# Token slots of 1024 columns in place of 1032, and pools shifted to multiples of 256 bytes, in a decoder layer on one Trainium2 core

## The chip, the core and the metric

The kernel runs on one core of one Trainium2 chip. The metric is the time of one execution on the device in microseconds (us); the time of a kernel is the median of its runs.

## What is computed

One decoder layer in float32 over 512 tokens of 2048 values, with weights that are used once each. The reference, cut to its frame:

```python
mod_all = einsum('bd,ldm->lbm', silu(c), w_ada) + b_ada        # six vectors of 2048
h = modulate(rms_norm(x, norm1_g), sh1, sc1)
u = h @ w_in                                                   # conv, queries, six key/value parts, gates
y_conv = short_conv_mixer(u_b, u_c, u_h, conv_w, conv_b)
k_cmp = compress(kv_heads(kc, True), cmp_pe_k, cmp_w1_k, cmp_w2_k)
v_cmp = compress(kv_heads(vc, False), cmp_pe_v, cmp_w1_v, cmp_w2_v)
y_attn = nsa_attention(q, k_cmp, v_cmp, k_slc, v_slc, k_win, v_win, gates)
mixed = concat([rms_norm(y_conv, gnorm_conv_g), rms_norm(y_attn, gnorm_attn_g)])
x = x + g1 * (mixed @ w_out)
h = modulate(rms_norm(x, norm2_g), sh2, sc2)
x = x + g2 * (square(relu(h @ w_ff1)) @ w_ff2)                 # 8192 hidden values
return rms_norm(x, normf_g)
```

`compress` turns windows of 32 tokens, 16 apart, into one key or value each: 31 windows, each a vector of 32 x 128 values, times a 4096 x 256 matrix, a gelu, and a 256 x 128 matrix.

## The kernel before

**Split matmuls.** Each float32 operand is held as two parts, `hi` (a rounded copy, made by ScalarE) and `lo` (the remainder, made by VectorE). `mm3` (L338) multiplies such a pair by another in three matmuls: hi by hi, hi by lo, lo by hi. For weights the parts are called `wh` and `wl`, or the two halves of a tile `hl`. In every matmul the weights, a 128 x 128 block, are loaded into the array by their own instruction, and the tokens, 512 or 256 columns, stream past.

**Stages.** The front (L344 to L871) computes the modulation vectors (192 loads of 512 KB, `wa`, each multiplied and summed on VectorE), the projections of `w_in`, the convolution and the compression. Its tokens stand in 16 tiles of 128 partitions: the first seven in the pool `side` (`h`), nine in slots (`h_m`). Weights come as raw blobs of 128 x 1024, or 128 x 1072 for the value projection, into three staging tiles `raw`, and are split into two pairs `wh`, `wl` by `weights` (L325). The attention stage (L874 to L1032) works on 8 heads and four blocks of 128 queries, with the output projection of the convolution half between, and ends with the first two blocks `w_oa`, staged the same way. The feed-forward stage (L1035 to the end) finishes the output projection and computes the two large matmuls by seven products on half blocks instead of eight, with 256 token columns in each matmul. It loads raw blobs into six tiles `rw` of 4096 bytes per partition and splits them into three tiles `hl` of 8192, two `sg` of 4096, or into `gt`. Its token tiles `tk` are slots again: in the first half of the stage the same 28 tiles serve all blocks; in the second half 14 new ones are loaded from DRAM for each of eight parts.

**Memory.** SBUF is handed out as a stack of pools, each tile padded to 32 bytes per partition. From the bottom: 16,512 bytes of scratch and constants of the framework, `consts` (`vec` of 1344 bytes first), `small`, then `mainp` with its 29 slots, each 128 x 1032 float32, 4128 bytes per partition. The slots begin at byte 34464 and end at 154176. Above come `attc` (`cst`, `ident_r`, `mask_r`, `kslc`, `vcmp` and small tiles, in the order in which the code makes them), `stage` (first three `raw` of 4288 bytes, then two `wh` and two `wl` of 4288) and `side`, whose place the pool `pa` takes in the attention stage. When `attc`, `stage` and `pa` are closed, the feed-forward's pool `ffp` starts at 154176, in the same bytes: six `rw`, three `hl` from 178752, `sg`, `gt`, `gb`, `p1`. A tile laid over an older one waits until the older one is done with. Seen modulo 256, the slots start at 160, 192, 224, 0, 32 and so on in turn, `hl`, `sg` and `gt` at 64, the two pairs `wh`, `wl` at (64, 192) and (0, 128), the side tiles `h` at 64.

**Order.** The class `Order` (L43) records all instructions of a stage, prices each by its operation and width, and plans in which order every engine issues them; a slot is given to the next tile when its last user is done. DMAs of weights are issued on SP's queue in that order. Tiles of the feed-forward are written by the same order with its own plan.

**Compression.** `compress` (L685) puts the 32 positions of all windows into two tiles `ct`, one for positions 0 to 15 and one for 16 to 31, each column group of 64 being the windows of both key/value groups for one position. It splits each into `chi` and `clo` and multiplies position after position. A weight load takes 66 columns, `m = slice((l % 16) * 64, (l % 16) * 64 + 66)`, and at the last position of a tile the two columns beyond the 1024 are read; the slot's columns 1024 to 1031 are set to zero for that (L691).

Of the kernel before, what the change touches and what calls it, by code (L numbers as in the profile page):

```python
# [9 lines left out]
F32 = mybir.dt.float32  # L10
F32R = mybir.dt.float32r
# [5 lines left out]
P = 128  # L17
T = 512
# [3 lines left out]
NG = 2  # L22
# [4 lines left out]
NEG = -1e30  # L27
SCALE = HD ** -0.5
BLOB = 1072
SLOT = 1032  # L30
NMAIN = 29
NSIDE = 7
NWA = 8
# [3 lines left out]
V_BADA, V_N1, V_CW, V_CB, V_GC, V_GA, V_N2, V_NF, V_C, V_ID, V_END = \  # L37
    0, 96, 112, 136, 144, 152, 160, 176, 192, 208, 336
C_COS, C_SIN, C_MASK, C_CMASK, C_ROW, C_END = 0, 512, 1024, 1152, 1280, 1281
# [230 lines left out]
def hybrid_layer(ctx: ExitStack, tc: tile.TileContext, a, out):  # L270
    nc = tc.nc
    PSUM = bass.MemoryType.PSUM

    consts = ctx.enter_context(tc.tile_pool(name="consts", bufs=1))
# [4 lines left out]
    attc = front.enter_context(tc.tile_pool(name="attc", bufs=1))  # L279
    stage = front.enter_context(tc.tile_pool(name="stage", bufs=2))  # L280

    def slot(dtype=F32, name="m"):
        return mainp.tile([P, SLOT], dtype, name=name, tag="m")

    def pair(dtype=F32, name="m"):
        return slot(dtype, name)[:, :2 * T].rearrange("p (a b) -> p a b", a=2)

    xs = [pair(name="x2") for _ in range(NK // 2)]
    nc = order = Order(tc, xs[0].tensor.tag, NMAIN, passes=6)
    ts = [small.tile([P, T], F32, name="t", tag="t", bufs=5) for _ in range(5)]  # L290
    scr, temps = ts[0].bitcast(BF16), cycle(ts[1:])
    accums = cycle([small.tile([P, T], F32, name="sacc", tag="acc2k", bufs=2) for _ in range(2)])
    wraw = cycle([stage.tile([P, BLOB], F32, name="raw", bufs=3) for _ in range(3)])
    whl = cycle([[stage.tile([P, BLOB], F32R, name=n) for n in ("wh", "wl")] for _ in range(2)])
    accs = cycle([small.tile([P, 2], F32, name="acc") for _ in range(4)])

    def temp(shape=(P, T), dtype=F32, name=None):
        t = next(temps)[:, :math.prod(shape[1:])].bitcast(dtype)
        if len(shape) == 4:
            return t.rearrange("p (a b c) -> p a b c", b=shape[2], c=shape[3])  # L300
        return t if len(shape) == 2 else t.rearrange("p (a b) -> p a b", b=shape[2])
# [23 lines left out]
    def weights(src, cols=1024, spare=False):  # L325
        raw = next(wraw)[:, :cols]
        nc.sync.dma_start(out=raw, in_=src)
        wh, wl = (slot(F32R, name="sw") for _ in range(2)) if spare else next(whl)
        wh, wl = wh[:, :cols], wl[:, :cols]
        nc.scalar.activation(wh, raw, AF.Copy)  # L330
        nc.vector.tensor_tensor(out=wl, in0=raw, in1=wh.bitcast(F32), op=OP.subtract)
        return wh, wl

    def split(dst, src):
        nc.scalar.activation(dst[:, 0], src, AF.Copy)
        nc.vector.tensor_tensor(out=dst[:, 1], in0=src, in1=dst[:, 0].bitcast(F32), op=OP.subtract)

    def mm3(ps, lh, ll, rh, rl, start, stop, more=False):  # L338
        nc.tensor.matmul(ps, lh, rh, start=start, stop=False, skip_group_check=more)
        nc.tensor.matmul(ps, lh, rl, start=False, stop=False, skip_group_check=more)  # L340
        nc.tensor.matmul(ps, ll, rh, start=False, stop=stop, skip_group_check=more)


    vec = consts.tile([P, V_END], F32, name="vec")  # L344
    nc.sync.dma_start(out=vec, in_=a["vec"][:, :V_END])
    ident = vec[:, V_ID:V_END]
    for i in range(NK // 2):
        nc.sync.dma_start(out=xs[i], in_=a["xt"][i])
    cst = attc.tile([P, C_END - C_MASK], F32, name="cst")
    cmask = cst[:, C_CMASK - C_MASK:C_ROW - C_MASK].rearrange("p (b n) -> p b n", b=NQ)  # L350
    rowv = cst[:, C_ROW - C_MASK:]
    ident_r = attc.tile([P, P], F32R, name="ident_r")
    mask_r = attc.tile([P, P], F32R, name="mask_r")
    rot = pair(name="rot")
    cos, sin = rot[:, 0], rot[:, 1]
    ones = consts.tile([P, P], F32, name="ones")
# [164 lines left out]
        yield 0.65  # L521

    kc, kwin = [], []
    kslc = [attc.tile([P, 2, 32 + T], F32R, name=f"kslc{g}") for g in range(NG)]

    def keys():

# [55 lines left out]
    for s, (name, k) in enumerate(steps[:-1]):  # L583
# [5 lines left out]
        wh, wl = w  # L589
# [50 lines left out]
    def other():  # L640
        return next(others)
# [36 lines left out]
        return ps  # L678


    vcmp = attc.tile([P, NG, 2, P], F32R, name="vcmp")
    cw2 = pair(name="cw2").rearrange("p a b -> p (a b)")[:, :576]
    nc.sync.dma_start(out=cw2, in_=a["vec"][:, V_END:])

    def compress(which, src):  # L685
        pe = cw2[:, which * 32:which * 32 + 32]
        w2 = [cw2[:, 64 + (which * 2 + i) * P:64 + (which * 2 + i + 1) * P] for i in range(2)]
        parts = []
        for hf in range(2):
            t = slot(name="ct")  # L690
            nc.vector.memset(t[:, 1024:SLOT], 0.0)  # L691
            tv = t[:, :1024].rearrange("p (l g n) -> p l g n", g=NG, n=32)
            n = 32 - hf
            for g in range(NG):
                nc.vector.tensor_tensor(
                    out=tv[:, :, g, :n],
                    in0=src[g].rearrange("p (n l) -> p l n", l=16)[:, :, hf:],
                    in1=pe[:, hf * 16:hf * 16 + 16, None].to_broadcast([P, 16, n]), op=OP.add)
            if hf:
                nc.vector.memset(tv[:, :, :, 31:], 0.0)  # L700
            hi = slot(F32R, name="chi")
            lo = slot(F32R, name="clo")
            nc.scalar.activation(hi, t, AF.Copy)
            nc.vector.tensor_tensor(out=lo, in0=t, in1=hi.bitcast(F32), op=OP.subtract)
            parts.append((hi, lo))
            if hf:
                w = weights(a["cmp_w1"][which * 8], spare=True)
            yield
        pc = other()
        for blk in range(8):  # L710
            wh, wl = w
            hi, lo = parts[blk // 4]
            for j in range(4):
                l = blk * 4 + j
                s = slice(j * 256, (j + 1) * 256)
                m = slice((l % 16) * 64, (l % 16) * 64 + 66)
                mm3(pc[:66, :256], hi[:, m], lo[:, m], wh[:, s], wl[:, s], l == 0, l == 31)
            if blk < 7:
                w = weights(a["cmp_w1"][which * 8 + blk + 1], spare=True)
            yield  # L720
        hid = temp([P, 256], name="hid")[:64]
        tt = temp([P, 256], name="htt")[:64]
        nc.scalar.activation(hid, pc[:64, :256], AF.Copy)
        nc.vector.tensor_tensor(out=tt, in0=hid, in1=hid, op=OP.mult)
        nc.vector.tensor_scalar(tt, tt, 0.044715, 1.0, op0=OP.mult, op1=OP.add)
        nc.vector.tensor_tensor(out=tt, in0=tt, in1=hid, op=OP.mult)
        nc.scalar.activation(tt, tt, AF.Tanh, scale=math.sqrt(2.0 / math.pi))
        nc.vector.tensor_scalar(tt, tt, 1.0, 0.5, op0=OP.add, op1=OP.mult)
        nc.vector.tensor_tensor(out=hid, in0=hid, in1=tt, op=OP.mult)
        pt = other()  # L730
        for i in range(2):
            nc.tensor.transpose(pt[:, i * 64:i * 64 + 64], hid[:, i * P:(i + 1) * P], ident[:64, :64])
        hidt = temp([P, 2, NG, 32], name="hidt")
        nc.scalar.activation(hidt.rearrange("p i g n -> p (i g n)"), pt[:, :P], AF.Copy)
        yield
        if which == 0:
            pk = other()
            for i in range(2):
                nc.tensor.matmul(pk[:, :64], w2[i], hidt[:, i].rearrange("p g n -> p (g n)"),
                                 start=i == 0, stop=i == 1)  # L740
            for g in range(NG):
                split(kslc[g][:, :, :32], pk[:, g * 32:g * 32 + 32])
        else:
            pad = temp([P, 2, NG, P], name="hpad")
            nc.vector.memset(pad, 0.0)
            nc.vector.tensor_copy(pad[:, :, :, :32], hidt)
            for g in range(NG):
                pv = other()
                for i in range(2):
                    nc.tensor.matmul(pv[:, :P], pad[:, i, g], w2[i], start=i == 0, stop=i == 1)  # L750
                split(vcmp[:, g], pv[:, :P])
# [6 lines left out]
    for j in range(8):  # L758
# [4 lines left out]
        for i in range(3):  # L763
            n = 3 * j + i
# [30 lines left out]
    for g in range(NG):  # L795
        pv = [bank() for _ in range(NQ)]
        for blk in range(4):
            wh, wl = weights(a["w_v"][g * 4 + blk], BLOB)
            more_ada(1)
            for j in range(4):  # L800
                k = blk * 4 + j
                s = slice(j * 268, (j + 1) * 268)
# [43 lines left out]
    for g in range(NG):  # L846
        pq = [bank() for _ in range(NR)]
        for k in range(NK):
            if k % 2 == 0:
                wh, wl = weights(a["w_q"][g * 8 + k // 2])  # L850
                more_ada(1)
                tick()
            for n in range(NR):
                s = slice((k % 2 * NR + n) * P, (k % 2 * NR + n + 1) * P)
# [28 lines left out]
    nc = tc.nc  # L883
    temps = cycle(ts)
    nc = order = Order(tc, mix[0].tensor.tag, NMAIN, passes=6)
# [113 lines left out]
    m = 2  # L999
# [35 lines left out]
    nc = order = Order(tc, x1[0].tensor.tag, NMAIN)  # L1035
# [57 lines left out]
    for k in range(8):  # L1093
        wh, wl = oa[k] if k < 2 else hilo(hl_tile(), raw_blob(a["w_oa"][k]))
        for i in range(8):
            s = slice(i * P, (i + 1) * P)
# [309 lines left out]
    for f in range(8):  # L1406
# [7 lines left out]
        for q in range(3 if last else 4):  # L1414
            raw = [raw_blob(a["w_f2"][4 * f + q, b]) for b in range(4)]
            ps = [{}, {}]
            for i, w in enumerate(operands(raw)):
# [3 lines left out]
                for j in range(2):  # L1421
                    mp = 2 * q + j
                    m = 2 * mp
# [119 lines left out]
```

## Time and profile before

| | |
|---|---|
| median of 3 runs | 2165.89 us |
| lowest and highest of them | 2164.7 and 2166.03 us |
| span of the profiled execution | 2163.4 us |

The span runs from the first instruction to the last of one profiled execution; the times of the runs hold what lies around it too. A page of the profile gives the busy time of each engine, then groups of instructions: the tile written, the tiles read, the shape, the count, the busy time and the mean length of one. All instructions that `Order` records carry its line, L116, so groups are told apart by the names of their tiles. Matmuls overlap: one of 512 columns is listed with some 0.39 us, one of 256 with 0.28, and the next starts before it ends. Their pace is therefore read from their starts, or from a count in a stretch. PE is TensorE's matmuls, PEld its weight loads, DVE VectorE, ACT ScalarE, POOL GpSimd, SP the engine that issues most DMAs.

### The profile page before, as it was taken

How to read it: one execution, taken by the hardware profiler on the slowest of the kernel's cores; microseconds unless marked ns; L12 is line 12 of the kernel's file. 1: busy time of each engine (PE TensorE's matmuls, PEld its weight loads, DVE VectorE, ACT ScalarE, POOL GpSimd, SP SyncE). 2: the span in 40 equal slices, each digit the busy share in tenths (PEclk: the TensorE clock that was granted, in tenths of full speed). 3: DMA queues.
4: the chain of work that ended last, by engine and by line, in shares of the span. 5: the costliest groups of instructions: out<-in, count | busy, mean ns of one | idle time of the engine just before them, and what ended most of it. 6: DMA issues, size and time to landing. Idle time of an engine off the chain costs nothing.

```text
span 2163.4 us, 37948 instructions
## 1 busy us (share of the span) xinstructions
PE 2107.7 (97%) x15014; PEld 1956.2 (90%) x15014; DVE 1891.8 (87%) x2975; ACT 1009.7 (47%) x1470; POOL 128.6 (6%) x244
## 2 busy tenths in 40 slices
PE   5999999999999999999999999999999999999997
PEld 3888777898777779999999999999999999999997
DVE  8989988887887547999999999999899999999997
ACT  4532333222555435766656665666433333333344
POOL 0000000000000001021112111111000000000000
PEclk8999999999999999999999999999999999999998
DMA  8996678888220144476666666668875366366342
GB/s 330 341 345 223 232 285 317 314 292 292 78 88 30 59 159 158 137 228 193 193 212 197 195 198 212 192 196 284 315 278 212 139 239 233 125 242 234 134 179 88
DMA packets 144129, 454.16 MB, mean 210 GB/s; under 512 B 15824, under 2 KB 20176, under 8 KB 143952
## 3 DMA queue, kind: packets, MB, share of 16 engines
q1 hardware_dynamic: 108816, 386.72, 50.1%
q0 software_dynamic: 34048, 63.98, 9.6%
q8 instruction: 118, 1.93, 0.4%
q10 hardware_dynamic: 1088, 1.05, 0.1%
q14 instruction: 59, 0.48, 0.1%
HBM read 383.53 MB, written 68.16 MB: 209 GB/s over the span
## 4 chain that ended last, share of the span: by engine, by line
PE 87%; DVE 7%; DMA 3%; issue 1%; ACT 1%; SPq 0%; DVEq 0%; ACTq 0%
PE pf L116 61%; PE ps L116 20%; PE pw L116 3%; PE pv L116 1%; DVE t L116 1%; DMA raw<-in_cmp_w 1%; PE s L116 1%; PE pt L116 1%; DVE nm L116 1%; DMA raw<-in_w_conv 1%; DVE wl L116 1%; DVE x L116 1%; DVE hl L116 1%; DVE p L116 0%; DMA rw<-in_w_f 0%
## 5 line engine op out<-in xcount | busy, mean ns | idle before, releaser
L116 PE MATMUL pf<-tk,hl 128*128 128x256 f32 x10704 | 1264.6, 280 | 1.2 <-DVE hl L116 0.7
L116 PEld LDWEIGHTS pf<-tk,hl 128*128 128x128 f32 x10704 | 1262.8, 188 | 1.8 <-DVE hl L116 0.9
L116 ACT ACTIVATE hl<-rw 128x1024 fp32r<-128x1024 f32 x269 | 284.7, 1059 | 354.6 <-PE pf L116 339.0
L116 DVE TENSOR_TENSOR hl<-rw,hl 128x1024 fp32r<-128x1024 f32 x269 | 327.9, 1220 | 52.2 <-ACT hl L116 52.1
L116 ACT ACTIVATE hl<-sg 128x1024 fp32r<-128x1024 f32 x180 | 191.1, 1062 | 247.5 <-PE pf L116 233.3
L116 DVE SCALAR_TENSOR_TENSOR t<-wa,cs 128x1024 bf16<-128x1024 f32 x192 | 234.5, 1221 | 21.7 <-DMA wa<-in_w_ada 19.2
L116 ACT ACTIVATE wh<-raw 128x1024 fp32r<-128x1024 f32 (+1 forms) x106 | 112.7, 1064 | 261.0 <-PE ps L116 222.1
L116 PE MATMUL ps<-h_m,wh 128*128 128x512 f32 x720 | 226.8, 394 | 0.0
L116 DVE TENSOR_TENSOR hl<-sg,hl 128x1024 fp32r<-128x1024 f32 x151 | 184.4, 1221 | 35.1 <-ACT hl L116 34.9
L116 PE MATMUL ps<-h,wh 128*128 128x512 f32 x560 | 179.4, 400 | 5.2 <-ACT h L116 3.2
L116 PEld LDWEIGHTS ps<-h_m,wh 128*128 128x128 f32 x720 | 134.8, 188 | 30.8
L116 DVE SCALAR_TENSOR_TENSOR x<-pf,mod,x 128x256 f32<-128x256 f32 (+1 forms) x280 | 134.6, 487 | 18.5 <-PE pf L116 17.8
L116 DVE TENSOR_TENSOR wl<-raw,wh 128x1024 fp32r<-128x1024 f32 (+1 forms) x106 | 129.9, 1226 | 23.3 <-ACT wh L116 22.8
L116 DVE TENSOR_TENSOR sg<-sg,rw 128x1024 f32<-128x1024 f32 x120 | 146.1, 1217 | 0.1
L116 PE MATMUL ps<-h_m,wl 128*128 128x512 f32 x360 | 141.8, 394 | 0.0
L116 PEld LDWEIGHTS ps<-h,wh 128*128 128x128 f32 x560 | 107.0, 192 | 32.7 <-ACT h L116 5.2
L116 POOL DMA_DIRECT2D g<-gt x192 | 101.5, 533 | 364.5 <-issue 179.2
L116 PE MATMUL ps<-h,wl 128*128 128x512 f32 x280 | 111.8, 399 | 0.0
L116 PE MATMUL pw<-mix,wh 128*128 128x512 f32 x256 | 86.7, 404 | 0.0
L116 PEld LDWEIGHTS ps<-h_m,wl 128*128 128x128 f32 x360 | 67.6, 188 | 15.8
L116 ACT ACTIVATE t<-t 128x512 f32<-128x512 f32 (+3 forms) x131 | 74.6, 571 | 13.0 <-DVE t L116 11.0
L116 DVE TENSOR_TENSOR sg<-rw 128x1024 f32<-128x1024 f32 x60 | 73.1, 1218 | 6.1 <-DMA rw<-in_w_f 3.2
(216 smaller groups left out, 2151.7 us busy)
## 6 DMA issues: line engine op xcount, KB each, us to landing
rw<-in_w_f SPq DMA_DIRECT2D x263, 512.0 KB, 3.8
wa<-in_w_ada SPq DMA_DIRECT2D x192, 512.0 KB, 6.2
tk<-g SPq DMA_DIRECT2D x114, 512.0 KB, 6.4
g<-gt POOLq DMA_DIRECT2D x192, 256.0 KB, 3.4
raw<-in_w_conv SPq DMA_DIRECT2D x32, 512.0 KB, 4.4
x<-in_xt SPq DMA_DIRECT2D x16, 512.0 KB, 6.1
raw<-in_w_kv SPq DMA_DIRECT2D x16, 512.0 KB, 4.9
raw<-in_w_cv SPq DMA_DIRECT2D x16, 512.0 KB, 3.6
```

Source lines behind the costliest of these rows:

```text
L116: x.i, x.eng, x.call = len(self.nodes), eng, (lambda: real(*args, **kw))
```

## The change

`SLOT` becomes 1024 columns, 4096 bytes. `vec` is padded from 336 to 424 columns, so that the slots begin at byte 34816, a multiple of 1024, and end at 153600. `kslc`, `vcmp`, `ident_r` and `mask_r` are made first in `attc`, `cst` is padded to 337 columns, staged tiles become 1088 columns wide (4352 bytes) of which 1072 are used, and `wh` and `wl` are made ahead of `raw`. With that `stage` begins at 169472 and the side tiles at 199936, both multiples of 256; `ffp` begins at 153600 and `hl` at 178176, multiples of 1024.

In `compress` the two columns past the end are no longer there: the memset goes, the copies take 1024 columns, and at positions 15 and 31 the weight load takes 64 columns and the matmul writes 64 rows instead of 66. In each block of four positions the last two change places, so that the accumulation ends with a position of 66 rows.

```diff
-SLOT = 1032
+SLOT = 1024
+WIDE = 1088
+VEC_W = 336 + 88
+CST_W = 1281 - 1024 + 80
...
-    wraw = cycle([stage.tile([P, BLOB], F32, name="raw", bufs=3) for _ in range(3)])
-    whl = cycle([[stage.tile([P, BLOB], F32R, name=n) for n in ("wh", "wl")] for _ in range(2)])
+    kslc = [attc.tile([P, 2, 32 + T], F32R, name=f"kslc{g}") for g in range(NG)]
+    vcmp = attc.tile([P, NG, 2, P], F32R, name="vcmp")
+    ident_r = attc.tile([P, P], F32R, name="ident_r")
+    mask_r = attc.tile([P, P], F32R, name="mask_r")
+    whl = cycle([[stage.tile([P, WIDE], F32R, name=n)[:, :BLOB] for n in ("wh", "wl")] for _ in range(2)])
+    wraw = cycle([stage.tile([P, WIDE], F32, name="raw", bufs=3)[:, :BLOB] for _ in range(3)])
...
-    vec = consts.tile([P, V_END], F32, name="vec")
+    vec = consts.tile([P, VEC_W], F32, name="vec")[:, :V_END]
...
-    cst = attc.tile([P, C_END - C_MASK], F32, name="cst")
+    cst = attc.tile([P, CST_W], F32, name="cst")[:, :C_END - C_MASK]
...
-            nc.vector.memset(t[:, 1024:SLOT], 0.0)
-            tv = t[:, :1024].rearrange("p (l g n) -> p l g n", g=NG, n=32)
+            tv = t.rearrange("p (l g n) -> p l g n", g=NG, n=32)
...
-            for j in range(4):
+            for j in (0, 1, 3, 2):
                 l = blk * 4 + j
                 s = slice(j * 256, (j + 1) * 256)
-                m = slice((l % 16) * 64, (l % 16) * 64 + 66)
-                mm3(pc[:66, :256], hi[:, m], lo[:, m], wh[:, s], wl[:, s], l == 0, l == 31)
+                rows = 66 if l % 16 < 15 else 64
+                m = slice((l % 16) * 64, (l % 16) * 64 + rows)
+                mm3(pc[:rows, :256], hi[:, m], lo[:, m], wh[:, s], wl[:, s], l == 0, l == 30)
```

More of the change, by code (lines that the diff above doesn't have):

```diff
@@ L348, in hybrid_layer @@
         nc.sync.dma_start(out=xs[i], in_=a["xt"][i])
-    cst = attc.tile([P, C_END - C_MASK], F32, name="cst")
+    cst = attc.tile([P, CST_W], F32, name="cst")[:, :C_END - C_MASK]
     cmask = cst[:, C_CMASK - C_MASK:C_ROW - C_MASK].rearrange("p (b n) -> p b n", b=NQ)
     rowv = cst[:, C_ROW - C_MASK:]
-    ident_r = attc.tile([P, P], F32R, name="ident_r")
-    mask_r = attc.tile([P, P], F32R, name="mask_r")
     rot = pair(name="rot")
@@ L523, in hybrid_layer @@
     kc, kwin = [], []
-    kslc = [attc.tile([P, 2, 32 + T], F32R, name=f"kslc{g}") for g in range(NG)]
     def keys():
@@ L678, in project @@
         return ps
-    vcmp = attc.tile([P, NG, 2, P], F32R, name="vcmp")
     cw2 = pair(name="cw2").rearrange("p a b -> p (a b)")[:, :576]
```

## The prediction, made before the change was run

> **What bounds the kernel now.** I read the page's busy line and its chain of work that ended last, then the view of stretches for the stages, then single stretches of TensorE's order of time.
>
> ```profile
> span 2163.4 us, 37948 instructions
> ...
> PE 2107.7 (97%) x15014; PEld 1956.2 (90%) x15014; DVE 1891.8 (87%) x2975; ACT 1009.7 (47%) x1470; POOL 128.6 (6%) x244
> ...
> PE 87%; DVE 7%; DMA 3%; issue 1%; ACT 1%; SPq 0%; DVEq 0%; ACTq 0%
> PE pf L116 61%; PE ps L116 20%; PE pw L116 3%; PE pv L116 1%; DVE t L116 1%; DMA raw<-in_cmp_w 1%; PE s L116 1%; PE pt L116 1%; DVE nm L116 1%; DMA raw<-in_w_conv 1%; DVE wl L116 1%; DVE x L116 1%; DVE hl L116 1%; DVE p L116 0%; DMA rw<-in_w_f 0%
> ```
>
> The reader is to see that 87% of the chain is TensorE itself, and that 61% is one group, the feed-forward matmuls into `pf`. The stretches below (busy time and count of PE, PEld, DVE, ACT, POOL, then clock, DMA share, GB/s) show it busy without a gap, at the full granted clock:
>
> ```profile
> 100.00:150.00 50.00, 50.00 (x217) 40.42 (x216) 44.77 (x79) 21.72 (x30) 0.00 (x0) 1.00 0.91 338
> ...
> 1000.00:1500.00 500.00, 500.00 (x4241) 500.00 (x4240) 455.93 (x609) 309.42 (x431) 94.69 (x179) 1.00 0.65 204
> ...
> 1560.00:2150.00 590.00, 589.08 (x4996) 588.64 (x4995) 551.56 (x789) 238.97 (x270) 2.64 (x5) 1.00 0.53 191
> ```
>
> 500 us over 4241 matmuls is 117.9 ns from start to start; 590 us over 4996 is 118.1. So the time is the number of matmuls times their pace, and only what changes the pace or the number can move it much. The groups, with their counts:
>
> ```profile
> L116 PE MATMUL pf<-tk,hl 128*128 128x256 f32 x10704 | 1264.6, 280 | 1.2 <-DVE hl L116 0.7
> ...
> L116 PE MATMUL ps<-h_m,wh 128*128 128x512 f32 x720 | 226.8, 394 | 0.0
> ...
> L116 PE MATMUL ps<-h,wh 128*128 128x512 f32 x560 | 179.4, 400 | 5.2 <-ACT h L116 3.2
> ...
> L116 PE MATMUL ps<-h_m,wl 128*128 128x512 f32 x360 | 141.8, 394 | 0.0
> ...
> L116 PE MATMUL ps<-h,wl 128*128 128x512 f32 x280 | 111.8, 399 | 0.0
> ...
> L116 PE MATMUL pw<-mix,wh 128*128 128x512 f32 x256 | 86.7, 404 | 0.0
> ```
>
> **Part 1, the pace: what addresses do to it.** The change keeps these matmuls and moves their operands. Before, a token slot is 4128 bytes, so the 29 slots start at all eight multiples of 32 modulo 256, while the feed-forward weight blocks (`hl`, `sg`, `gt`) start at 64 modulo 256 every time. Call *offset* the address of a token tile minus that of the weights, modulo 256. Here are runs of six matmuls on one token slot (columns: start, us from first start to last end, group, count):
>
> ```profile
> 1072.48 0.84 PE L116 MATMUL pf<-tk,hl 128*128 128x256 f32 x6
> 2063.69 0.84 PE L116 MATMUL pf<-tk,hl 128*128 128x256 f32 x6
> 1521.20 0.88 PE L116 MATMUL pf<-tk,hl 128*128 128x256 f32 x6
> 2118.88 0.88 PE L116 MATMUL pf<-tk,hl 128*128 128x256 f32 x6
> 900.37 0.86 PE L116 MATMUL pf<-tk,hl 128*128 128x256 f32 x6
> 938.66 0.87 PE L116 MATMUL pf<-tk,hl 128*128 128x256 f32 x6
> 2147.49 0.88 PE L116 MATMUL pf<-tk,sg 128*128 128x256 f32 x6
> ```
>
> One matmul lasts 0.28, so five steps take 0.56 in the first two rows and 0.60 in the next two: 112 and 120 ns by rounded figures, 113.3 and 120.0 by the trace's starts. Clock, shape and engine are alike; the slots differ. The first pair is the first and last of 26 runs at offset 192 in which every step is 113.3. The second is the first and last of 24 runs at offset 0 (slot 5) in which, after a first step of 117, every step is 120.0. Rows six and seven are the first and last of all 228 runs at offset 0 (slots 5, 13, 21). Over all 1754 runs of six (900.37 the first, 2147.49 the last), the steps behind the first average, by offset: 0 118.7; 32 117.7; 64 117.6; 96 119.4; 128 119.5; 160 118.0; 192 116.2; 224 118.5.
>
> It is the offset and not the token address alone. In the projections two weight buffers alternate, at (`wh`, `wl`) = (0, 128) and (64, 192) modulo 256. First and last start of three blocks of 24 matmuls:
>
> ```profile
> 110.43 0.62 PE L116 MATMUL ps<-h,wh 128*128 128x512 f32 x2
> ...
> 115.79 0.40 PE L116 MATMUL ps<-h,wl 128*128 128x512 f32 x1
> ...
> 205.21 0.62 PE L116 MATMUL ps<-h_m,wh 128*128 128x512 f32 x2
> ...
> 210.57 0.39 PE L116 MATMUL ps<-h_m,wl 128*128 128x512 f32 x1
> ...
> 116.02 0.63 PE L116 MATMUL ps<-h,wh 128*128 128x512 f32 x2
> ...
> 121.33 0.39 PE L116 MATMUL ps<-h,wl 128*128 128x512 f32 x1
> ```
>
> The first has tokens at 64 and weights at (0, 128), the second tokens at 128 and weights at (64, 192): both offsets (64, 192), both 5.36 us over 23 steps, 233.0 ns. The third has tokens at 64 like the first, weights at (64, 192), offsets (0, 128): 5.31 over 23, 230.9. Same offsets, same pace; same token address, other pace.
>
> After the change every slot starts at a multiple of 1024, `hl`, `sg` and `gt` too (the 29 slots end at 153600, six raw blobs of 4096 later `hl` begins), staged weights and the side tiles `h` at multiples of 256. So the offset is 0 everywhere, one of the eight mixed before, and never disturbed by a change of slot.
>
> What does offset 0 settle to? The pace has a memory: a run depends on what came before, and each new slot starts it afresh, so most runs of six show the way there. Where steps repeat without a change they are 113.3 (17 x 6.67 ns), 120.0 (18 x 6.67), or a pattern of three that sums to 353.3 (53 x 6.67, 117.8 each). At offset 0 the only one seen to hold is 120.0: 24 runs of slot 5. The commoner way through offset 0 (117, 118, 119, 121, 117, 118, as in the 938.66 run) is cut off by the next slot. Three runs in slot 21 that come from steps of 120 pass its last members, 121, 117, 117, and go on 120, 120, 120; first and last of them:
>
> ```profile
> 1771.77 0.88 PE L116 MATMUL pf<-tk,hl 128*128 128x256 f32 x6
> 1811.46 0.88 PE L116 MATMUL pf<-tk,hl 128*128 128x256 f32 x6
> ```
>
> The common way thus leads to 120.0 as well, where it is not cut off. I take 120.0 for all: 10,704 x (120.0 - 117.9) = **+22.5 us**. Bounds: 113.3, the fastest that holds anywhere, gives 10,704 x -4.6 = -49.2 us; above, 120.0 is also the slowest that holds.
>
> **Part 2, 512 columns.** Blocks of 24 at one and the same offset for both weight halves occur with `hl`:
>
> ```profile
> 788.85 5.76 PE L116 MATMUL pf<-mixa,hl 128*128 128x512 f32 x24
> ...
> 800.05 5.76 PE L116 MATMUL pf<-mixa,hl 128*128 128x512 f32 x24
> ...
> 811.26 5.76 PE L116 MATMUL pf<-mixa,hl 128*128 128x512 f32 x24
> ```
>
> Offsets 224, 64 and 192, and (5.76 - 0.39) / 23 = 233.5 each time. The three mixed blocks above average (233.0 + 233.0 + 230.9) / 3 = 232.3. After, both halves have one offset: +1.2 ns on 720 + 560 + 360 + 280 + 256 = 2176 matmuls, **+2.6 us**. Bounds: twice the 256-column steps, 226.7 and 240: -12 and +17 us.
>
> The Trainium skill, page "TensorE: Matmul & The Clock Gate", section "Step-by-step: what each phase is for", says that TensorE has two independent SBUF read ports and that loading the next weights takes no read bandwidth from the running matmul. By it, parts 1 and 2 would be nothing; the runs of 113.3 and 120.0 ns of one instruction disagree. It is the second rival.
>
> **Part 3, the small edits** in `compress`:
>
> ```profile
> L116 DVE MEMSET ct<- 128x8 f32 x4 | 0.3, 65 | 0.0
> ...
> L116 DVE TENSOR_TENSOR clo<-ct,chi 128x1032 fp32r<-128x1032 f32 x4 | 4.9, 1232 | 0.0
> ...
> L116 ACT ACTIVATE chi<-ct 128x1032 fp32r<-128x1032 f32 x4 | 4.3, 1065 | 6.5 <-DVE ct L116 6.3 <-DVE y L116 0.2
> ```
>
> Four memsets of 65 ns go; eight copies lose 8 of 1032 columns (9 ns each). Together -0.3 us at most, beside a busy TensorE. For positions 15 and 31, weight loads have 64 columns instead of 66, six in all per call, and the last two positions swap: no step moves. Price 0, bounds -0.3 and 0. The planner sees slightly other durations and could order the front otherwise; I price that 0 within +-4, the size of a DMA or two on the chain. DVE's own pace does not ask for alignment: its 1032 columns take 1232 ns, 1.19 a column, the same as the 1220 for 1024 in `hl`.
>
> **Part 4, who lies under whom.** Feed-forward tiles reuse the memory of attention's. Before, the second and third raw blobs of the feed-forward lie on staged raw weights, free early; after, on `wh` of the first two `w_oa` blocks, still read until TensorE ends those blocks:
>
> ```profile
> 782.34 0.73 PE L116 MATMUL pf<-mixa,hl 128*128 128x512 f32 x2 [0.91 <-ACT hl L116]
> 783.60 5.42 PE L116 MATMUL pf<-mixa,hl 128*128 128x512 f32 x22 [0.53 <-DVE hl L116]
> ...
> rw<-in_w_oa SPq DMA_DIRECT2D x14, 512.0 KB, 4.3
> ...
> L116 ACT ACTIVATE hl<-rw 128x1024 fp32r<-128x1024 f32 x269 | 284.7, 1059 | 354.6 <-PE pf L116 339.0
> L116 DVE TENSOR_TENSOR hl<-rw,hl 128x1024 fp32r<-128x1024 f32 x269 | 327.9, 1220 | 52.2 <-ACT hl L116 52.1
> ```
>
> So block k = 3 is loaded from 781.4 (782.34 less the 0.91 waited), and SP holds the later blobs behind it. 781.4 + 4.3 + 1.06 + 1.22 = 788.0; it is needed at 788.85. Hidden with 0.9 us to spare: price 0. If that cover goes (landings up to 2 or 3 us longer), TensorE waits 1 to 2 us once, and again as much if the blob behind is late. The two waits of 0.91 and 0.53 stay, since `hl` still lies on weights of `w_oa`. Bounds -1.4 and +3.
>
> **Transfers.** The Trainium skill, page "DMA: Bandwidth & Descriptors", section "How a descriptor splits into AXI transactions", says that a descriptor not starting at a multiple of 256 bytes costs a transaction more: 17 for 16 on a 4096-byte row. By it, as an estimate, the chain's 3% DMA, 65 us, would shrink by 1/17, and the sum by 3.8 us; no view here splits landings by address. I leave it out of the sum.
>
> **Sum.** +22.5 + 2.6 + 0 + 0 = +25.1 on the execution's own 2163.4: 2188.5. The median shown, 2165.89, lies 2.5 above this span, so **2191**.
>
> **Rivals.**
> - *Offset 0 never settles*, or waits throw it out again, and it keeps the 118.7 of its unsettled steps: 10,704 x 0.8 = +8.6, with 2.6: 2177. For it: most of the 228 runs; against it: nothing disturbs the offset any more.
> - *It settles to a pattern of three at 117.8*, as offsets 32, 64 and 192 do, or operands do not contend: 10,704 x -0.1 = -1, with 0 to 2.6: 2165 to 2168, no change. Against it: not seen at offset 0. This is also where the page's rule of two ports ends.
> - *Faster: it settles to 113.3.* The 113.3 runs at slot 27 and its like all have the token slot itself at a multiple of 256, what the change gives every slot. If that decides, and not the difference to the weights, 10,704 matmuls gain 4.6 ns: -49.2 + 2.6, 2119; the point of decision is whether steps of 113.3 repeat past the first hundred. Against it: the three blocks of 512 columns, where the difference decided.
> - *The change doesn't do what it says*: the pools do not shift as reckoned, the weights' slots stay mixed: 2166.
>
> **How the numbers follow.** Settled at 120.0: 0.48 (2191, with 2186 to 2197 by parts 3 and 4). Unsettled: 0.15. Pattern of three or no contention: 0.17. 113.3: 0.17. No shift: 0.03. A measurement of this kernel can tell about 0.2%, 4.3 us, from no change. Slower by more: 0.48 + 0.15 = 0.63; within: 0.17 + 0.03 = 0.20; faster: 0.17. The range runs from no change to the settled case with part 2 near its upper bound, 2160 to 2202, and leaves out the fast case. Cases of both signs do hold chance, but the slow ones most: alone 2174 to 2200.
>
> **What would show it.** In the changed kernel 1000 to 1500 us should hold 4167 matmuls (500 / 0.120) instead of 4241, and runs of six on any slot should take 0.88. If 4245 are there, the pattern of three holds; 4410 mean 113.3. Blocks of 24 in the projections should take 5.76. The wait before block k = 3 near 789 tells of part 4. The prediction is wrong if the steps are alike but not 120.0, or if they still vary from slot to slot: then address bits above 256 bytes matter too.

## The result, and the profile after

| | before | changed | ratio |
|---|---|---|---|
| median | 2165.96 us | 2177.14 us | 1.0058, 95% interval 1.0043 to 1.0072 |
| lowest and highest of 4 runs | 2164.7 and 2166.84 | 2175.97 and 2180.49 | |
| span of the profiled execution | 2163.4 | 2176.1 | |

The change made the kernel slower by 0.6%, 11 us. The prediction was 2191, slower, with a range of 2160 to 2202. The direction and the main mechanism held, but the loss is less than half of the 25 us forecast. One term of the sum had the wrong sign, and with it the front accounts for 11 of the 14 us between 2191 and 2177.

First the page of the changed kernel, with the lines that answer to those of before:

```profile
span 2176.1 us, 37941 instructions
...
PE 2121.7 (98%) x15014; PEld 1979.9 (91%) x15014; DVE 1899.1 (87%) x2971; ACT 1006.3 (46%) x1470; POOL 128.2 (6%) x244
...
PE 81%; DVE 4%; DMA 2%; ACT 1%; issue 1%; SPq 0%; DVEq 0%; ACTq 0%
PE pf L119 64%; PE ps L119 11%; PE pw L119 3%; PE pv L119 1%; DMA wa<-in_w_ada 1%; PE s L119 1%; PE pt L119 1%; DVE nm L119 1%; DMA raw<-in_cmp_w 1%; DVE t L119 0%; DVE wl L119 0%; DVE p L119 0%; DVE tt L119 0%; DVE x L119 0%; DVE sw L119 0%
```

The same 15,014 matmuls keep TensorE busy 14 us longer. The feed-forward's share of the chain has grown from 61 to 64%. (The chain is traced less far here, its shares add up to 89% in place of 99%, so the smaller share of `ps` tells nothing.) What the two stages do is read from the view of stretches:

```profile
100.00:150.00 50.00, 50.00 (x222) 41.40 (x221) 45.75 (x84) 20.82 (x27) 0.00 (x0) 1.00 0.94 347
1000.00:1500.00 500.00, 500.00 (x4169) 500.00 (x4169) 451.42 (x599) 303.08 (x426) 91.79 (x174) 1.00 0.64 199
1560.00:2150.00 590.00, 590.00 (x4919) 590.00 (x4918) 547.59 (x774) 235.66 (x261) 2.63 (x5) 1.00 0.54 189
```

In the projections 222 matmuls pass in 50 us where 217 passed before. In the feed-forward 4169 pass in 500 us where 4241 passed. The clock is 1.00 in all of them, as before. (A window also counts the matmuls in flight at its edges, about two.)

Where the stages begin, and how long the long runs take, is read from TensorE's order of time (start, us from the first start to the last end, group, count, wait ahead of it). First the kernel before:

```profile
866.31 2.98 PE L116 MATMUL pf<-tk,hl 128*128 128x256 f32 x24
...
918.86 640.18 PE L116 MATMUL pf<-tk,hl 128*128 128x256 f32 x5426
1559.72 572.78 PE L116 MATMUL pf<-tk,hl 128*128 128x256 f32 x4858 [0.69 <-DVE hl L116]
```

And the changed kernel:

```profile
110.44 0.62 PE L119 MATMUL ps<-h,wh 128*128 128x512 f32 x2
...
115.65 0.39 PE L119 MATMUL ps<-h,wl 128*128 128x512 f32 x1
...
774.01 0.73 PE L119 MATMUL pf<-mixa,hl 128*128 128x512 f32 x2 [1.15 <-ACT hl L119]
775.27 41.12 PE L119 MATMUL pf<-mixa,hl 128*128 128x512 f32 x214 [0.53 <-DVE hl L119]
...
857.86 3.04 PE L119 MATMUL pf<-tk,hl 128*128 128x256 f32 x24
...
911.27 1234.24 PE L119 MATMUL pf<-tk,hl 128*128 128x256 f32 x10284
```

- The matmuls on `tk` begin at 857.86 instead of 866.31: the stages ahead of them **gain 8.45 us**.
- From there to the end it takes 2176.1 - 857.9 = 1318.2 us instead of 2163.4 - 866.3 = 1297.1: the feed-forward **loses 21.1 us**. The sum, +12.7, is the difference of the spans.
- The last row is one run of 10,284 matmuls without a wait, (1234.24 - 0.28) / 10,283 = 120.0 ns from start to start. Before, the two runs have (640.18 - 0.28) / 5425 = 117.95 and (572.78 - 0.28) / 4857 = 117.9.
- A block of 24 matmuls of 512 columns takes 115.65 - 110.44 = 5.21 us over its 23 steps, 226.5 ns. The blocks of before took 5.31 to 5.36.

So one and the same layout, offset 0, is the slow one for 256 columns and the fast one for 512.

### The profile page after: what moved, and what is told of

The parts are those of the page before. It is cut to its first block, busy times and chain, and to the rows that moved or that the text cites. A ratio compares the mean times of both kernels' runs of the same rounds, so it can differ in the third digit from the quotient of the medians.

```text
span 2176.1 us, 37941 instructions
## 1 busy us (share of the span) xinstructions
PE 2121.7 (98%) x15014; PEld 1979.9 (91%) x15014; DVE 1899.1 (87%) x2971; ACT 1006.3 (46%) x1470; POOL 128.2 (6%) x244
## 3 DMA queue, kind: packets, MB, share of 16 engines
q10 hardware_dynamic: 1088, 1.05, 0.1%
## 4 chain that ended last, share of the span: by engine, by line
PE 81%; DVE 4%; DMA 2%; ACT 1%; issue 1%; SPq 0%; DVEq 0%; ACTq 0%
PE pf L119 64%; PE ps L119 11%; PE pw L119 3%; PE pv L119 1%; DMA wa<-in_w_ada 1%; PE s L119 1%; PE pt L119 1%; DVE nm L119 1%; DMA raw<-in_cmp_w 1%; DVE t L119 0%; DVE wl L119 0%; DVE p L119 0%; DVE tt L119 0%; DVE x L119 0%; DVE sw L119 0%
## 5 line engine op out<-in xcount | busy, mean ns | idle before, releaser
L119 PE MATMUL pf<-tk,hl 128*128 128x256 f32 x10704 | 1286.8, 283 | 0.5 <-ACT t L119 0.5
L119 PEld LDWEIGHTS pf<-tk,hl 128*128 128x128 f32 x10704 | 1285.4, 192 | 0.8 <-ACT t L119 0.7
```

Source lines behind the costliest of these rows:

```text
L119: x.i, x.eng, x.call = len(self.nodes), eng, (lambda: real(*args, **kw))
```

## Experiments

Three theories stood open. **A**: the difference of the two addresses modulo 256, the offset, sets the pace, and an undisturbed offset falls into a cycle that repeats. **C**: the address of the token slot itself counts, or something else of the aligned layout. **Others** for the front: cheaper edits in `compress`, another order by the planner, transfers that land earlier.

### The edits of `compress` alone, on the kernel before

```diff
-            t = slot(name="ct")
-            nc.vector.memset(t[:, 1024:SLOT], 0.0)
+            t = slot(name="ct")[:, :1024]
...
-            for j in range(4):
+            for j in (0, 1, 3, 2):
...
+                rows = 66 if l % 16 < 15 else 64
```

> The kernel before, addresses untouched, with the edits of `compress` alone: no memset, 1024 columns in ct, chi and clo, 64 rows at positions 15 and 31, the last two positions of each four swapped. If these edits are worth nothing: 2166, the front ends within 1 us of before. Rival (the planner, which prices them anew, orders the front otherwise, and part of the front's 8 us is that): up to 8 us faster, 2158.

Measured: 2164.99 us over 10 runs, ratio 0.9998 (0.9988 to 1.0008). The edits are worth nothing that shows in the time. In its profile the matmuls on `tk` begin 3.9 us ahead of before:

```profile
862.37 2.99 PE L116 MATMUL pf<-tk,hl 128*128 128x256 f32 x24
```

The feed-forward then gives 3 of them back. Its addresses aren't quite those of before: the planner gave some token tiles other slots (by the addresses of the two programs, 1116 instead of 1392 of the 10,704 matmuls stand at offset 0, and 1026 instead of 552 at 128), and its feed-forward steps average 118.2 ns, not 117.9. The 3.9 us of the front are mostly shorter waits ahead of the compression. TensorE's idle time before its matmuls on `chi` (releaser: us, times), in the kernel before:

```profile
  ACT sw L116: 4.5, 4
  DVE ct L116: 1.1, 1
```

with the edits alone:

```profile
  ACT sw L116: 1.7, 2
  DVE sw L116: 0.6, 1
```

and in the changed kernel:

```profile
  ACT sw L119: 4.2, 3
  DVE sw L119: 1.2, 2
```

5.6, 2.3 and 5.4 us: the changed kernel doesn't have this gain, so it is no part of its 8.45 us. In the eight profiles of this study that have offset 0 in the front, the matmuls on `tk` begin between 857.86 and 860.13; single executions thus differ by some 2 us there.

### Every address moved by 64 bytes, no difference changed

```diff
-VEC_W = 336 + 88
+VEC_W = 336 + 88 + 16
```

> The changed kernel with `vec` 64 bytes wider, so that slots, staged weights, raw blobs, side tiles and all tiles of the feed-forward begin at 64 modulo 256: every difference is as in the changed kernel, every address itself is moved. Theory A (differences): the same pace everywhere, 4169 matmuls in 1000 to 1500 us, front steps of 226.7, 2177. Rival C (a token slot at a multiple of 256 counts by itself): front and feed-forward steps as mixed as before, 117.9 and 232, some 2166. Rival D (DMA destinations off 256 bytes cost more): matmul steps as in the changed kernel, but later landings in the front, up to 4 us, 2181.

Measured: 2180.14 us (2179.5 to 2183.46), ratio to before 1.0070 (1.0055 to 1.0085). The stretch of the feed-forward:

```profile
1000.00:1500.00 500.00, 500.00 (x4169) 500.00 (x4169) 451.30 (x600) 302.87 (x426) 91.80 (x174) 1.00 0.63 199
```

4169 again, to the matmul: 64 bytes that move both operands change nothing, so the address itself doesn't count. Theory C falls. That the difference does count is shown by the next two runs, which move one operand alone. The time is near rival D's 2181, but the intervals of the two ratios overlap (up to 1.0072 for the changed kernel, from 1.0055 here), so the 3 us can't be told from noise, and landings don't tell of them either (DMA issues: tile, queue, count, KB each, us to landing), in this kernel:

```profile
rw<-in_w_f SPq DMA_DIRECT2D x263, 512.0 KB, 3.7
...
raw<-in_w_kv SPq DMA_DIRECT2D x16, 512.0 KB, 5.4
```

and in the changed kernel, where `raw` and `rw` begin at multiples of 256:

```profile
rw<-in_w_f SPq DMA_DIRECT2D x263, 512.0 KB, 3.7
...
raw<-in_w_kv SPq DMA_DIRECT2D x16, 512.0 KB, 5.3
```

Other medians differ both ways (`in_cmp_w` 4.2 here and 3.9 there, `in_w_q` 3.9 and 4.5). A small cost of landings is not excluded.

### Offset 192 in the projections alone

```diff
+    stage.tile([P, 16], F32, name="gap0", bufs=1)
     whl = cycle([[stage.tile([P, WIDE], F32R, name=n)[:, :BLOB] for n in ("wh", "wl")] for _ in range(2)])
     wraw = cycle([stage.tile([P, WIDE], F32, name="raw", bufs=3)[:, :BLOB] for _ in range(3)])
+    stage.tile([P, 48], F32, name="gap1", bufs=1)
```

> The changed kernel with `wh`, `wl` (and `raw`) 64 bytes higher, side tiles 256 bytes higher, feed-forward as in the changed kernel: offset 192 in the projections alone. Theory A (the difference sets the pace, and the front's gain of 8 us is the step of 512 columns going from 232 to 226.7 at offset 0): projections at 233.3 as in blocks of offset 192 before, 1920 x 6.1 = +11.7, 2189; 1000 to 1500 us holds 4169 as in the changed kernel. Rival C (the front gained by aligned tokens, aligned DMA landings or another order): projections stay at 227, 2177.

Measured: 2186.81 us (2185.38 to 2187.48), ratio to before 1.0097 (1.0082 to 1.0112). Its stretches, and the begin of the matmuls on `tk`:

```profile
100.00:150.00 50.00, 50.00 (x216) 40.30 (x215) 45.13 (x79) 21.62 (x30) 0.00 (x0) 1.00 0.92 337
1000.00:1500.00 500.00, 500.00 (x4169) 500.00 (x4168) 451.99 (x599) 301.19 (x423) 93.39 (x177) 1.00 0.61 196
```

```profile
867.42 3.04 PE L119 MATMUL pf<-tk,hl 128*128 128x256 f32 x24
```

216 in place of 222, and 867.42 in place of 857.86: 64 bytes cost the front 9.6 us, more than it had gained, with the edits of `compress` left as in the changed kernel. Its steps in the projections are 233.3, as theory A has it, slower than the 231.9 of the mixed offsets before; some 3 of the 11.7 us expected come back because TensorE waits 2.5 us ahead of the compression's matmuls on `chi`, not 5.4. The feed-forward stays at 4169. So the front's gain is the pace of the 512 columns at offset 0.

### Offset 192 in the feed-forward alone

```diff
     rw = cycle([ffp.tile([P, 1024], F32, name="rw", bufs=6) for _ in range(6)])
+    ffp.tile([P, 16], F32, name="gap", bufs=1)
     hl = cycle([ffp.tile([P, 2, 1024], F32R, name="hl", bufs=3) for _ in range(3)])
```

> The changed kernel with 64 unused bytes between `rw` and `hl`: feed-forward weights at 64 modulo 256, token slots stay at 0, so the offset there is 192; the front keeps offset 0. Theory A (the difference of the two addresses modulo 256 sets the pace, and 192 settles at the 113.3 ns seen in single runs before): 1000 to 1500 us holds 4410 matmuls, 10,704 x -6.7 = -71 us, 2106. Rival B (192 keeps its mean of before, 116.2, even undisturbed): 4303 matmuls, -41 us, 2136. Rival C (not the difference but the token slot's own address at a multiple of 256, or something else of the aligned layout, makes the 120.0): 4169 matmuls, 2177.

Measured: 2153.22 us, ratio to before 0.9919 (0.9888 to 0.9949), but the eight runs fall into two groups: 2136.1, 2136.9 and 2138.2, and five from 2152.5 to 2159.0. The profile is of a run of 2153.98:

```profile
1000.00:1500.00 500.00, 500.00 (x4248) 500.00 (x4247) 454.76 (x609) 309.41 (x431) 93.99 (x179) 1.00 0.65 207
```

```profile
901.04 3.91 PE L119 MATMUL pf<-tk,hl 128*128 128x256 f32 x32 [0.47 <-ACT t L119]
904.85 3.09 PE L119 MATMUL pf<-tk,sg 128*128 128x256 f32 x24
...
910.61 1211.74 PE L119 MATMUL pf<-tk,hl 128*128 128x256 f32 x10284
```

None of the three counts came; 4248 is the pattern of three, 117.8 ns. (Rival B's time, 2136, was met by three runs, but no stretch of this profile holds its 116.2.) But the 113.3 is there too: of the 31 steps behind the wait at 901.04, three take 220, 124 and 118 ns, and the other 28 are 113 or 114: 0.46 + 28 x 0.1133 = 3.63 us, the row's 3.91 less the 0.28 of its last matmul. From the trace's starts, the feed-forward from 864.84 us consists of pure stretches: 301 steps at 117.8, the 28 at 113.3, 5472 at 117.8, then 20 and 44 at 113.3, 4839 at 117.8. No stretch changes its cycle by itself; between two of them there is always a break, a longer step (0.76 us at 900.29, 0.22 at 904.85, 0.22 at 1549.68, 0.33 at 1552.41, 0.25 at 1557.94). Offset 192 has two cycles, and a break throws the dice. The runs of 2136 would then be those in which one of the long stretches fell on 113.3 (4839 x 4.45 ns = 21.5 us less, before what new waits take of it). This is inferred from their time; there is no profile of such a run.

### Sweeps: every offset in one kernel

`hl` tiles got 256 bytes more, and the begin of the 1024 columns in use moves every few blocks:

```diff
-        return t[:, 0], t[:, 1]
+        a, b = [(-o % 256) // 4 for o in now[0]]
+        if a <= b:
+            return t[:, a:a + 1024], t[:, 1024 + b:2048 + b]
+        return t[:, 1024 + a:2048 + a], t[:, b:b + 1024]
...
     def ff1(p):
+        now[0] = FIRST[(p - 3) * 8 // 29]
...
     for f in range(8):
+        now[0] = SECOND[f]
```

> The changed kernel with `hl` tiles 256 bytes longer, of which the 1024 columns in use begin at a place that changes eight times in each half of the feed-forward: offsets 0, 32, 64, 96, 128, 160, 192, 224 in the first half, 128, 64, 224, 192, 160, 32, 0, 96 in the second, undisturbed for some 600 to 1400 matmuls each. Theory A (the difference modulo 256 sets the pace, and an undisturbed offset falls into a cycle that repeats): 0 gives 120.0 twice, 192 gives 113.3 or 117.8 in each of its stretches and nothing between, 32 and 64 give 117.8 (64 perhaps 113.3), and 96, 128, 160, 224 one repeating cycle each, between 113.3 and 120.0. Rival E (not the offset but the stretch of the kernel, its data or transfers, sets the pace): paces follow the place in the kernel, and the same offset differs between its two stretches by more than the step from 113.3 to 117.8.

Measured: 2160.88 us, one run. Stretches of 50 us, PE alone (busy time, count, clock, DMA share, GB/s): offsets 32, 64 and 192 in the first half, then 64, 192, 32 and 0 in the second.

```profile
1030.00:1080.00 50.00, 50.00 (x431) 1.00 0.61 194
1090.00:1140.00 50.00, 50.00 (x427) 1.00 0.61 195
1380.00:1430.00 50.00, 50.00 (x427) 1.00 0.62 200
...
1600.00:1650.00 50.00, 50.00 (x427) 1.00 0.36 123
1760.00:1810.00 50.00, 50.00 (x444) 1.00 0.40 133
1920.00:1970.00 50.00, 50.00 (x431) 1.00 0.38 131
2000.00:2050.00 50.00, 50.00 (x419) 1.00 0.36 122
```

The reader is to see 431 twice for offset 32 and 427 twice for 64, at DMA shares of 0.6 and of 0.4: the stretch of the kernel and its transfers don't matter. And 427 and 444 for offset 192, its two cycles. All stretches, mean step in ns from the trace's starts (504 to 1248 matmuls each):

| offset | 0 | 32 | 64 | 96 | 128 | 160 | 192 | 224 |
|---|---|---|---|---|---|---|---|---|
| first half | 120.0 | 116.7 | 117.8 | 120.0 | 118.7 | 118.7 | 117.8 | 118.3 |
| second half | 120.0 | 116.7 | 117.8 | 120.0 | 118.7 | 120.0 | 113.3 | 118.3 |

Six of the eight offsets have one pace in both halves, and none differs by more than the step from 113.3 to 117.8, so rival E falls. Offset 0 is one of the two that give 120.0 both times. Offsets 160 and 192 each show two cycles; for 160 theory A had one.

> As the run above, with offsets that are no multiples of 32: 16, 48, 80, 112, 144, 176, 208, 240 in the first half, 240, 8, 200, 184, 176, 48, 112, 16 in the second. If memory is read in pieces of 32 bytes, an offset of 16 behaves as 0 or 32 and so on, and 200 as 192; if finer, cycles appear that no multiple of 32 shows. The interest is in an offset that gives 113.3 alone.

Measured: 2166.07 us, one run. Means: 8: 117.6; 16: 120.0 and 117.3; 48: 116.7 twice; 80: 118.1; 112: 118.3 and 120.0; 144: 120.0; 176: 118.8 twice; 184: 118.3; 200: 117.8; 208: 123.3; 240: 118.3. No offset gives 113.3 alone, and pieces of 32 bytes don't explain it: 208 is slower than any multiple of 32 (steps of 117 and 130 ns in turn), 8 isn't at the 120.0 of offset 0, and 184 has neither pace of 192. The search for a better single offset gave nothing.

> As above, with different offsets for the two halves of the weights (hi, lo): (192,0), (0,192), (192,64), (64,192), (192,128), (128,0), (0,128), (192,32) in the first half, (192,160), (160,192), (192,224), (224,192), (64,0), (0,64), (32,192), (64,128) in the second. Theory A: three matmuls go with one token block, two with hi and one with lo, so the pace is a cycle of three steps, near two parts hi and one part lo: (192,0) 115.6 or 118.5, (0,192) 117.8 or 119.3. Rival: the offsets of the two halves do not add up, and some pair settles at 113.3 from every start.

Measured: 2158.1 us, one run. Two stretches of it, (192, 64) and (64, 192):

```profile
1095.00:1145.00 50.00, 50.00 (x444) 1.00 0.68 216
1160.00:1210.00 50.00, 49.82 (x440) 1.00 0.66 206
```

Both hold 113.3 (the second has a short wait inside). The others: (192,0), (0,192), (64,0) and (0,64) 117.8; (192,128) 118.2; (128,0) 118.3; (0,128) 119.1; (192,32) 117.0; (32,192) 119.2; (192,160) 118.1; (160,192) 118.9; (192,224) 120.0; (224,192) 118.7; (64,128) 115.6. The halves don't add up as two parts hi and one part lo: (192,0) was to give 115.6 or 118.5. Here (192,160) is the mean of two paces, 117.8 and, behind a break, 118.9. (192,64) began with steps of 118, 122, 118, 115 and 120 and then fell into 113.3, which made it worth a kernel of its own.

### The pair (192, 64), and its mirror

```diff
-    hl = cycle([ffp.tile([P, 2, 1024], F32R, name="hl", bufs=3) for _ in range(3)])
+    ffp.tile([P, 16], F32, name="gap", bufs=1)
+    hl = cycle([ffp.tile([P, 2, 1056], F32R, name="hl", bufs=3)[:, :, :1024] for _ in range(3)])
```

The mirror differs in its gap: 48 columns in place of 16.

> The changed kernel with 64 unused bytes ahead of `hl` and halves of `hl` 1056 columns apart, of which 1024 are used: hi weights at 64, lo weights at 192 modulo 256, tokens at 0, offsets (192, 64) in the whole feed-forward; the front keeps offset 0. Theory (this pair has one cycle only, 113.3, as in its one undisturbed stretch so far, which began with other steps and fell into it): 1000 to 1500 us holds 4412 matmuls, 10,704 x -6.7 = -71 us from the changed kernel, 2106 in every run. Rival (it has the second cycle of 117.8 too, as 192 alone has, and a stall chooses): runs between 2106 and 2154.

> The same with the two halves exchanged: hi weights at 192, lo weights at 64, offsets (64, 192). Theory: 113.3 here too, as in its one undisturbed stretch, 2106 in every run. Rival: 113.3 and 117.8 both hold, 2106 to 2154.

The pair: **2117.35 us**, five runs from 2116.6 to 2118.7, ratio to before **0.9775** (0.9762 to 0.9788), to the changed kernel 2117.35 / 2177.14 = 0.973. It is faster than both. Its stretch and its long runs:

```profile
1000.00:1500.00 500.00, 500.00 (x4414) 500.00 (x4413) 467.60 (x630) 317.87 (x442) 93.88 (x178) 1.00 0.70 223
```

```profile
860.12 2.90 PE L119 MATMUL pf<-tk,hl 128*128 128x256 f32 x24
...
937.27 566.43 PE L119 MATMUL pf<-tk,hl 128*128 128x256 f32 x4992 [0.30 <-DVE hl L119]
1503.97 24.79 PE L119 MATMUL pf<-tk,hl 128*128 128x256 f32 x216 [0.27 <-DVE hl L119]
1530.54 547.30 PE L119 MATMUL pf<-tk,hl 128*128 128x256 f32 x4812 [1.78 <-DVE hl L119]
```

(566.43 - 0.28) / 4991 = 113.4 ns. Behind each of the waits a few other steps stand (at 1504.19 us 117, 120, 120, 117, 119, 121, 116), and then 113.3 again, every time: here the break doesn't matter. The time came out 11 us above the 2106 expected. The pace is not the reason, the waits are. TensorE's waits from 850 us to the end, in this kernel (releaser; us in total, times, longest):

```profile
PE pf L119 <- DVE sacc L119: 3.4, 2, 1.9
PE pf L119 <- DVE hl L119: 2.6, 4, 1.8
PE pf L119 <- ACT t L119: 1.4, 1, 1.4
PE pf L119 <- DVE t L119: 1.1, 1, 1.1
PE pf L119 <- DVE x L119: 0.6, 1, 0.6
```

9.1 us together; the same view of the changed kernel has 3.7. With what a wait costs beside its idle time (steps above 135 ns: after the longest one, of 2.06 us, fifteen steps take some 0.21 us each), the feed-forward waits some 9 us more than in the changed kernel, by the trace's starts, and its matmuls on `tk` begin 2.3 us later (860.12). Of the 5.4 us that the view has more, 2.6 are waits for VectorE's split of `hl`, which is now late four times, 1.9 are for `sacc` and 0.9 for `t`.

The mirror: four runs, 2115.97 once and 2163.15 to 2166.07 three times. The profiled one, of 2164.61, holds

```profile
1000.00:1500.00 500.00, 500.00 (x4208) 500.00 (x4207) 455.25 (x605) 306.76 (x428) 92.87 (x176) 1.00 0.64 204
```

4208: a cycle of six steps with a mean of 118.9. It has 113.3 as well: by the trace's starts, 238 steps from 911.24 us on, until a single step of 168 ns at 938.21 throws it into the other, where it stays to the end of the 10,284. The rival held for it, with 118.9 as the second pace, and the theory for the pair. That the run of 2115.97 kept 113.3 is inferred from its time. Which half lies where thus matters, though both orders contain the same two offsets. That the pair has no second cycle is what one profile and five runs show, and not more.

### The sweep for 512 columns

```diff
+        if cols == 1024 and not spare:
+            staged[0] += 1
+            o = (-32 * (staged[0] // 6) % 256) // 4
...
-        wh, wl = wh[:, :cols], wl[:, :cols]
+        wh, wl = wh[:, o:o + cols], wl[:, o:o + cols]
```

> The changed kernel with staged weights of 1024 columns beginning at a place in their tile that moves by 32 bytes after every six blobs: offsets 0, 32, 64 and on to 224 in the matmuls of 512 columns, twice around, 144 matmuls to a stretch. Theory A (the offset sets the pace of 512 columns too, by another table than for 256): 0 at 226.7 both times, 192 at 233.3 as in the run with 64 bytes, 64 and 224 near 233.5 as in the three blocks before, 32, 96, 128 and 160 between 226.7 and 240, the same in both rounds. Rival (0 is not special, all aligned fronts are at 227): 227 at every offset.

Measured: 2182.93 us, one run. Two stretches of 30 us, offset 64 and offset 128:

```profile
99.00:129.00 30.00, 30.00 (x133) 24.62 (x132) 27.91 (x49) 14.88 (x21) 0.00 (x0) 1.00 0.94 347
...
166.00:196.00 30.00, 30.00 (x130) 24.15 (x129) 29.81 (x44) 7.89 (x10) 0.00 (x0) 1.00 0.52 190
```

Mean steps from the trace's starts, without those that waited, both times around:

| offset | 0 | 32 | 64 | 96 | 128 | 160 | 192 | 224 |
|---|---|---|---|---|---|---|---|---|
| first | 228.1 | 233.3 | 228.9 | 233.4 | 233.3 | 234.3 | 233.1 | 233.2 |
| second | 227.9 | 233.2 | 229.0 | 233.3 | 233.3 | 233.9 | 232.7 | 233.1 |

Offset 0 is the fastest of all eight for 512 columns (226.7 where nothing has just broken the run), so the rival falls. 64, for which theory A had 233.5, is the only other one below 232. The other six stand between 232.7 and 234.3. The three blocks that the prediction had, at 224, 64 and 192, were a sample of the common value; and at 64 even that block was not at the pace that longer stretches hold.

## Why the prediction was right, and where it was not

- **Part 1, the pace of 256 columns: right, in mechanism and size.** Forecast: every step 120.0, 4167 matmuls in 1000 to 1500 us, +22.5 us. Measured: 120.0 over 10,284 matmuls, 4169, and +21.1 from the first matmul on `tk` to the end. The missing 1.4 is mostly a wait that went: the 0.69 for `hl` at 1559.72 is gone, and steps above 135 ns cost 4.8 us beyond a normal step in place of 6.0. (That slower matmuls leave the weights more time would explain it; no run tests it.) The two steps of the argument that were inference are now shown. Offset and not address: by the run with every address moved and the runs with one moved. The way into 120.0: in the changed kernel the steps from 905.65 on are 117, 118, 117, 118, 119, 121, 117, 117 and then 120, and in the sweeps offset 0 came to 120.0 every time.
- **Part 2, 512 columns: the step that failed.** The term of +1.2 ns on 2176 matmuls, +2.6 us, took the 233.5 of blocks at offsets 224, 64 and 192 for the pace at any single offset. At offset 0 it is 226.7. By the trace's starts, the steps of the projections fell from 231.9 to 227.2 on 1920 matmuls, those of `pw` from 232.2 to 230.6 on 384, and those of `mixa` from 233.2 to 226.8 on 192: 9.0 + 0.6 + 1.2 = 10.8 us less, of which 2.3 came back as longer waits in the projections (steps above 262 ns: 17.5 us beyond a normal step in place of 15.2). Measured at the end of the front: -8.45 in place of +2.6. The lower bound that the prediction gave, 226.7 and -12, came close to what was measured. There was no row at offset 0 in the profile of before, except as one half of a mixed pair; and of the two pairs, (64, 192) with 233.0 and (0, 128) with 230.9, the one with offset 0 was the faster, a sign that was read past. A step that is taken from three offsets to a fourth one, when part 1 has just shown that offsets differ, deserved a rival of its own.
- **Part 3, small edits: right.** 0 within what can be told: 0.9998 (0.9988 to 1.0008). That they also move token tiles to other slots, and with them the mix of offsets, was not thought of; in the changed kernel, where every offset is 0, it can't matter.
- **Part 4, who lies under whom: right.** The row at 775.27 runs over 214 matmuls, so block k = 3 was loaded in time; ahead of k = 2 TensorE waited 1.15 + 0.53 where it had waited 0.91 + 0.53.
- **Sum.** 2191 less 11.05 (part 2 and all else in the front), less 1.4 (part 1), less 1.5 (the median lies 1.0 above the span, not 2.5) is 2177. That lies below the 2186 to 2197 of the settled case, whose mechanism held; a range from 2160 to 2202, which takes in no change at all, had room for the error in part 2.
- **Rivals.** "Offset 0 never settles" gave 2177, the time that was measured, and is nevertheless wrong: 118.7 would have put 4212 matmuls into the window, not 4169. Two errors would have met at the right number. The fast rival, that the slot's own address decides, falls with the run in which every address moves. That operands don't contend, the rule of two independent read ports in the Trainium skill (page "TensorE: Matmul & The Clock Gate", section "Step-by-step: what each phase is for"), would, as we infer from it, have left the time alone; here moving the weights by 64 bytes, or their halves, moved the whole kernel from 2177 to 2187, 2153 or 2117.
- **Transfers, left out of the sum: rightly.** By the rule of the Trainium skill (page "DMA: Bandwidth & Descriptors", section "How a descriptor splits into AXI transactions") that a transaction starts at a multiple of 256 bytes, a row of 4096 bytes that starts off such a multiple takes 17 of them, not 16, as an estimate worked out from the rule. No cost of it shows in the landings of `rw`: at 64 modulo 256 their median is 3.7 us, at 0 it is 3.7.

What stays open: why an offset has the cycle that it has. The runs give a table, not a model of the memory, and the table for 256 columns doesn't carry over to 512.

## What to carry to other kernels

When a kernel is bound by back-to-back matmuls, read the pace from the starts and compare tiles at different addresses: a few per cent can hang on where weights and moving operand lie relative to each other, and "aligned" is just one of the cases, here the best for one width and nearly the worst for another. A sweep in one kernel, with a view that slides inside a slightly longer tile, prices many placements in a single run, though a stretch shows only one of the cycles that its placement may have. Prefer a placement to which the pace returns behind every wait over one that is as fast but has a second cycle, since the latter can give another time in the next run.

## What the runs showed of the hardware

- At the offsets of the first sweep, undisturbed matmuls settle at steps that sum to a whole number of 6.67 ns after a few of them: 113.3 is 17, 120.0 is 18, 116.7 is 35 for two steps, 117.8 is 53 for three, 118.3 is 71 for four, 118.7 is 89 for five. A pace held for 10,284 matmuls without a change; in the profiles of the changed kernel, of offset 192, of the pair and of its mirror it changed only behind a longer step (168 ns is the shortest) or where the offset or the weights' tile changed.
- One placement can have two such cycles (offset 192: 113.3 and 117.8, both in one profile). It is the likely reason why that program takes some 2136 or some 2154 us, and the mirror of the pair 2116 or some 2165, where the slower runs had no lower granted clock (0.993 and 0.994, against 0.991).
- The pace answers to 16 and even 8 bytes (offset 192: 113.3 or 117.8; 208: 123.3. Offset 0: 120.0; 8: 117.6, in one stretch).
